# A hybrid attention and expert block on one Trainium2 core: all 40 modulation weight tiles of the first part are multiplied and summed by VectorE, and none by Pool

## Chip, cores and metric

The kernel runs on one core of one Trainium2 chip. The metric is the device time of one execution in microseconds; the kernel before was timed in three runs, and their median stands for it. One more execution was profiled, and all rows come from that one.

## What is computed

The reference is one block on 256 tokens of width 1024. Cut to its main lines:

```
ada = silu(c) @ w_ada + b_ada                     # w_ada: 1024 x 6144, the modulation
shift1, scale1, gate1, shift2, scale2, gate2 = split(ada, 6)
h = rms_norm(x) * (1 + scale1) + shift1
qa, ka, va, qb, kb, vb = split(h @ w_in)
mixed = concat(rms_norm(windowed_attention(qa, ka, va)), rms_norm(neighbourhood_attention(qb, kb, vb)))
x = x + gate1 * (mixed @ w_out)
h2 = rms_norm(x) * (1 + scale2) + shift2
x = x + gate2 * peer(h2)                          # 8 heads choose 16 of 16384 experts for each token
out = rms_norm(x) * final_g
```

Everything is float32. `ada` is a product of one vector with a matrix: six parts of eight column groups, 48 tiles of 128 outputs by 1024 inputs.

## The kernel before

**Tiles and parts.** Features lie on the 128 partitions, eight chunks of them, and tokens run along the free axis. A modulation tile has an output on each partition and the 1024 inputs along the free axis. The first part of the kernel makes 40 of the 48 tiles (all but gate2, whose eight tiles come late in the second part), the input projection (18 weight tiles), attention in eight pairs of heads, the output projection (8 tiles), the second norm and the first products of the expert queries. The second part does the remaining queries, the choice of experts, and runs over 128 tiles of the first and 128 tiles of the second expert matrix; beside these, for 96 tokens, single expert rows are fetched by indirect DMAs of Pool's queue.

**A modulation tile** (`load_ada`, lines 592 to 607). `ca` holds silu(c), the same 1024 numbers on every partition. On VectorE one `scalar_tensor_tensor` with `accum_out` multiplies the tile by `ca` and leaves the sum in one column of `ada` (lines 606 and 607). For the 15 tiles in the table `ON_POOL` (line 39), Pool multiplies the tile by `ca` in place (line 598), and ScalarE then adds up the row by an `activation` with `accum_out` (line 601). The 15 belong to gate1, scale2 and shift2, so the 16 tiles of scale1 and shift1 are on VectorE already.

**Weight tiles of the projections.** `load_w` loads a tile, ScalarE rounds it to its high half (line 626), and VectorE or Pool subtracts that from it for the low half (`lo`, line 630). TensorE multiplies the halves in three terms (lines 442 and 806).

**What sets the order.** The first part is written as jobs with the engines they may run on, each with a cost, what it depends on and which buffers it takes. A planner (`plan`, `forward`, `backward`) orders them: a list scheduler that is run 300 times with disturbed priorities from a fixed seed, and of which the order with the earliest end of TensorE is kept. Jobs with several engines are the split's subtraction (VectorE or Pool), evictions from PSUM (ScalarE or VectorE: the projection at line 851 or 853, turned values at 870 or 872, turned probabilities at 1007 or 1009, attention's output at 1032 or 1034), the weighing of the softmax (line 982 for VectorE and Pool, 979 for ScalarE) and additions (540 and 1081, VectorE or Pool). Each engine's instructions are then written down in that order, and every engine works its own queue strictly in order. Weights are loaded by SP's queue, in the planner's order, into 8 buffers of one kind and 9 of another; a load stands at the head of SP's queue until its buffer is free. In the second part the order is written by hand, with a count of each engine's assumed time for VectorE's side work.

**Other lines that are named below.** 945: VectorE adds the bias to the scores and takes the extreme from PSUM. 962, 968 and 973: small sums and reciprocals of the softmax. 949: ScalarE's exponential. 750: the sums of squares over the partitions on TensorE. 1077: the output projection times gate and norm, from PSUM. 1557 and 1507: the products of the two expert matrices.

Of the kernel before, what the change touches and what calls it, by code (L numbers as in the profile page):

```python
# [12 lines left out]
AF = mybir.ActivationFunctionType  # L13
# [3 lines left out]
P = 128  # L17
D = 1024
NC8 = 8
# [16 lines left out]
NCST = _o  # L36

SHIFT1, SCALE1, GATE1, SHIFT2, SCALE2, GATE2 = range(6)
ON_POOL = {(GATE1, 0), (GATE1, 2), (GATE1, 3), (GATE1, 5), (GATE1, 7), (SCALE2, 0), (SCALE2, 1), (SCALE2, 2), (SCALE2, 4), (SCALE2, 5), (SCALE2, 6), (SHIFT2, 1), (SHIFT2, 2), (SHIFT2, 3), (SHIFT2, 4)}
RAW = 4  # L40
SETTLE = 6.0
SETS = (64, 32)
# [17 lines left out]
LO_POOL = 1  # L60
# [5 lines left out]
def kernel(ctx: ExitStack, tc: tile.TileContext, xT, crow, vecs, cst, w_ada, w_in, w_out,  # L66
# [11 lines left out]
    V, S, PE, G = nc.vector, nc.scalar, nc.tensor, nc.gpsimd  # L78
# [7 lines left out]
    ada = keep.tile([P, 6, 8], F32, name="ada")  # L86
# [3 lines left out]
    cs = keep.tile([P, 8], F32, name="cs")  # L90
# [54 lines left out]
    def add(alts, *deps, take=(), free=(), lag=0.0, after=None, rows=P):  # L145
        return Job(alts, deps, take, free, lag, after, rows)
# [174 lines left out]
    MM = 0.1095  # L321
# [16 lines left out]
    tiles = {}  # L338
# [125 lines left out]
    ca = carve(D)  # L464
# [52 lines left out]
    def silu(y, x):  # L517
        S.activation(y, x, AF.Exp, scale=-1.0)
        V.tensor_scalar(y, y, 1.0, None, op0=ALU.add)
        V.reciprocal(y, y)  # L520
        V.tensor_mul(y, y, x)

    silu(c8t[:8], c8[:8])
    for w, part in ((0, SCALE1), (1, SCALE2)):
        a0 = VEC["b_ada"][0] + part * 8
        V.scalar_tensor_tensor(gb[:, w, :], vec[:, a0:a0 + 8], 1.0, v_("g2" if w else "g1"),
                               op0=ALU.add, op1=ALU.mult)
# [19 lines left out]
    cas = []  # L547
    for w in range(2):
        key = ("ca", w)
# [6 lines left out]
        m = add([("pe", 0.86, spread_c)], take=[("bank", key)], rows=8)  # L556
# [33 lines left out]
    column = {}  # L590

    def load_ada(part, c):
        key = ("ada", part, c)
        m = load(w_ada[part, c], key)
        col = ada[:, part, c:c + 1]
        if (part, c) in ON_POOL:
            def mul():
                G.tensor_mul(tiles[key], tiles[key], ca)

            def total():  # L600
                S.activation(tiles[key], tiles[key], AF.Copy, accum_out=col)

            m = add([("pool", 2.3, mul)], m, *cas)
            column[part, c] = add([("act", 1.04, total)], m, free=[key])
        else:
            column[part, c] = add([("dve", 1.15, lambda: V.scalar_tensor_tensor(
                tiles[key], tiles[key], 1.0, ca, op0=ALU.mult, op1=ALU.mult, accum_out=col))], m, *cas, free=[key])

    halved = {}
# [4 lines left out]
    def load_w(kind, i):  # L614
        key = ("w", kind, i)
        m = load(SRC[kind][i], key)
        hkey = ("h", kind, i)
        held_key[kind, i] = hkey
        if (kind, i) in WHOLE or kind == "q" and i < NQ:
            halved[kind, i] = whole[kind, i] = m  # L620
            held_key[kind, i] = key
            return

        def high():
            halves[kind, i] = new_halves(got(hkey))
            S.activation(halves[kind, i][0], tiles[key].rearrange("p (c n) -> p c n", n=P), AF.Copy)

        def low(e):
            hi, lo = halves[kind, i]
            e.tensor_sub(lo, tiles[key].rearrange("p (c n) -> p c n", n=P), hi.bitcast(F32))  # L630

        a = add([("act", 0.95, high)], m, take=[("split", hkey)])
        halved[kind, i] = add([("dve", 1.14, lambda: low(V))] + [("pool", 2.3, lambda: low(G))] * LO_POOL, a, free=[key])


    lscr = dram.tile([8, 512], F32, name="lscr")
# [1 line left out]
    def line_mm():  # L638
        PE.matmul(take_bank("line").rearrange("p a b -> p (a b)")[:8, :], t5s[:32], onehs[:32], start=True, stop=True)

    m = add([("pe", 0.86, line_mm)], take=[("bank", "line")], rows=32)
    m = add([("dve", 0.65, lambda: V.tensor_add(line[:8], tiles["line"].rearrange("p a b -> p (a b)")[:8, :], maska[:8]))],
            m, free=["line"])
# [122 lines left out]
    m = None  # L766
    for i in range(4):
        a = add([op("act", c_act(512), S.activation, sq[:, 2 * i:2 * i + 2, :], xs[:, 2 * i:2 * i + 2, :],
                    AF.Square)], xin[i])
        if i:  # L770
            a = add([op("dve", c_dve(512), V.tensor_add, sq[:, 0:2, :], sq[:, 0:2, :], sq[:, 2 * i:2 * i + 2, :])], a, m)
        m = a
    m = add([op("dve", c_dve(256), V.tensor_add, sq[:, 0, :], sq[:, 0, :], sq[:, 1, :])], m)
    m = ssum("n1", sq[:, 0, :], m)
# [3 lines left out]
    for c in range(NC8):  # L778
        x = add([op("pool", c_pool(256), G.tensor_mul, xr[:, c, :], xs[:, c, :], ny),
                 op("dve", c_dve(256), V.tensor_mul, xr[:, c, :], xs[:, c, :], ny)], scaled)  # L780
        a = add([op("dve", 0.08, V.scalar_tensor_tensor, mod[:, 0, c:c + 1], ada[:, SCALE1, c:c + 1], v_("g1", c),
                    gb[:, 0, c:c + 1], op0=ALU.mult, op1=ALU.add)], column[SCALE1, c])
# [33 lines left out]
    m = None  # L816
    for c in range(NC8):
        if KT == 16:
            for k in range(2):
                m = kouter(("in", 2 * c + k), [(c, n) for n in range(8 * k, 8 * k + 8)], m, hready[c])  # L820
            continue
        i = 3 * (c // 2) + c % 2
        m = kouter(("in", i), [(c, n) for n in range(8)], m, hready[c])
        if c % 2:
            m = kouter(("in", i + 1), [(b, n) for b in (c - 1, c) for n in range(8, 12)], m, hready[c], hready[c - 1])
# [53 lines left out]
    for i in range(KT, 18):  # L879
        key = ("in", i)  # L880

        def win(i=i, key=key):
            products_of(take_bank(key)[:, 0, :], operands(("in", i), xr), ALL)

        m = add([("pe", tile_cost(("in", i)), win)], halved["in", i], *hready, take=[("bank", key)],
                free=[held_key["in", i]])
# [12 lines left out]
    for u in range(8):  # L899
        q, k, vn, bias, j = pair_names(u)  # L900
# [18 lines left out]
        def score(u=u, q=q, k=k, skeys=skeys):  # L919
            ps = [take_bank(x) for x in skeys]  # L920
            for b in range(2 if u < 4 else 4):
# [10 lines left out]
                take=[("bank", x) for x in skeys] + [("pb", pkey)], rows=64 if GA else 50)  # L932
        previous = chain(previous, s, PACE)
        for b in ((0, 2, 1, 3) if GA else range(4)):
# [17 lines left out]
            a = add([("dve", 0.42 if GA else 0.285, shifted)], s, bias_in, free=[skeys[b % 2 if GA else 0]])  # L952
# [4 lines left out]
        if GA:  # L957
# [12 lines left out]
            a = add([("dve", 0.15, sink1)], *ttrs)  # L970
            a = add([("act", 0.2, sink2)], a)
            last = [add([("dve", 0.1, sink3)], a, *exps)]
        a = add([("dve", 0.15, lambda st_=st_: V.reciprocal(st_()[:, 3, :], st_()[:, 1, :]))], *last)
# [17 lines left out]
        for half, norm in enumerate(norms):  # L991
# [12 lines left out]
            def kept(eng, tkey=tkey, ckey=ckey):  # L1004
# [3 lines left out]
                else:  # L1008
# [4 lines left out]
                             take=[("ptb", ckey)], free=[tkey]))  # L1013
# [624 lines left out]
def _layout(np, i):  # L1638
    def cols(v):
        return v.reshape(-1, P).T  # L1640

    def tiles(w):
        return w.reshape(8, P, -1, P).transpose(2, 1, 0, 3).reshape(-1, P, D)

    pa = np.array([j + 4 * s for j in range(4) for s in range(2)])
    fa = (pa[:, None] * 64 + np.arange(64)[None]).reshape(-1)
    vec = np.concatenate([
        cols(i["c"][0]),
        i["b_ada"][0].reshape(6, 8, P).transpose(2, 0, 1).reshape(P, 48),
        cols(i["norm1_g"][0]), cols(i["norm2_g"][0]), cols(i["final_g"]),  # L1650
        cols(i["out_norm_a"][0][fa]), cols(i["out_norm_b"][0]),
        np.broadcast_to(i["sink_a"][0][pa][None], (P, 8)),
    ], axis=1)
    w_in = i["w_in"][0]
    order = [np.arange(512, 640)] + [fa[j * P:(j + 1) * P] for j in range(4)] + [np.arange(640, 768)]
    for j in range(4):
        for s in range(3):
            order.append(768 + 512 * s + j * P + np.arange(P))
    w_in = tiles(w_in[:, np.concatenate(order)]).reshape(18, P, 8, P)
    first = []  # L1660
    for cp in range(4 if KT == 12 else 0):
        for c in (2 * cp, 2 * cp + 1):
            first.append(w_in[0:8, :, c].transpose(1, 0, 2))
        first.append(w_in[8:12, :, 2 * cp:2 * cp + 2].transpose(1, 2, 0, 3).reshape(P, 8, P))
    for c in range(8 if KT == 16 else 0):
        for k in range(2):
            first.append(w_in[8 * k:8 * k + 8, :, c].transpose(1, 0, 2))
    w_in = np.concatenate([np.stack(first), w_in[KT:]]).reshape(18, P, D)
    w_out = i["w_out"][0]
    w_out = np.concatenate([w_out[:512][fa], w_out[512:]], axis=0)  # L1670
    w_out = w_out.reshape(2, 4, P, 4, 2, P).transpose(0, 3, 2, 4, 1, 5).reshape(8, P, D)
    rpb = np.stack([i["rpb_b"][0].reshape(4, 2, 465)[:, :, 108 + 31 * r:264 + 31 * r] for r in range(4)])
    rpb = rpb.transpose(2, 0, 1, 3).reshape(-1)
    return {
        "xT": i["x"][0].T.reshape(8, P, T).transpose(1, 0, 2),
        "crow": i["c"].reshape(8, P),
        "vecs": vec,
        "cst": _constants(np),
        "w_ada": i["w_ada"][0].T.reshape(6, 8, P, D),
        "w_in": w_in,  # L1680
        "w_out": w_out,
        "w_query": tiles(i["w_query"][0]),
        "t5": i["t5_table"][:, pa],
        "rpb": rpb,
        "skT": i["sub_keys"][0].reshape(16, P, P).transpose(2, 0, 1),
        "uT": i["u_experts"][0].reshape(NE, P, 8, P).transpose(0, 3, 2, 1).reshape(NE, P, D),
        "uE": i["u_experts"][0],
        "vE": i["v_experts"][0],
    }
# [20 lines left out]
```

## Time and profile before

| | us |
|---|---|
| Median of three runs | 851.04 (849.75 to 851.42) |
| Profiled execution | 850.8 |
| Its span, first to last instruction | 849.0 |
| TensorE busy in it | 775.2 |
| VectorE busy | 593.1 |
| ScalarE busy | 268.0 |
| Pool busy | 330.6 |

The span is what the rows of the trace add up to; the execution's own time lies 1.8 us over it. The busy times are averages over stages with different limits, so a stage has to be read by itself. A VectorE row's time is that of the instruction from its start to its end, with what it waited for inside the engine counted in; waiting for a semaphore before the start is counted as idle.

### The profile page before, as it was taken

What the parts mean: (1) busy time and instruction counts of PE and PEld (TensorE: products, weight loads), DVE (VectorE), ACT (ScalarE), POOL (GpSimd) and SP (SyncE); (2) the same over time, 40 slices, a digit from 0 to 9 for tenths busy, and PEclk for the clock granted to TensorE, in tenths of its full rate; (3) what the DMA queues carried; (4) which work ended last, traced back from release to release, by engine and by line L of the source; (5) the groups of instructions that cost most, each with busy time, mean ns of one, the idle gap of its engine ahead of it and who ended that gap; (6) DMA issues with size and microseconds to landing.
All of it is one profiled execution on the core that took longest, in us unless ns stands there. A gap on an engine that the chain in (4) does not pass through costs nothing.

```text
span 849.0 us, 15375 instructions
## 1 busy us (share of the span) xinstructions
PE 775.2 (91%) x5846; PEld 753.9 (89%) x5846; DVE 593.1 (70%) x1308; ACT 268.0 (32%) x741; POOL 330.6 (39%) x271
## 2 busy tenths in 40 slices
PE   3998786789799999999999999999999989899894
PEld 1997575689799999999999999999999988899893
DVE  6999999887677999569998775644435444453534
ACT  4456675456231112179876521000000000000003
POOL 2545686456314436412233233533333333332300
PEclk9999998999999999999999999999999999999997
DMA  8995666095768999999999999999999999999951
GB/s 328 408 328 206 223 227 234 0 348 202 259 229 297 392 413 395 416 413 361 359 378 374 401 371 416 415 412 416 415 416 415 414 415 416 415 413 418 414 205 50
DMA packets 81212, 289.27 MB, mean 341 GB/s; under 512 B 9281, under 2 KB 10825, under 8 KB 81010
## 3 DMA queue, kind: packets, MB, share of 16 engines
q1 hardware_dynamic: 36352, 125.60, 38.5%
q0 software_dynamic: 27776, 100.79, 30.2%
q10 hardware_dynamic: 17010, 61.89, 18.4%
q8 instruction: 46, 0.75, 0.4%
q14 instruction: 28, 0.23, 0.1%
HBM read 287.18 MB, written 1.07 MB: 340 GB/s over the span
## 4 chain that ended last, share of the span: by engine, by line
PE 34%; DMA 28%; issue 5%; DVE 3%; POOL 3%; ACT 0%; DVEq 0%; ACTq 0%; POOLq 0%
PE b L1507 27%; DMA row<-in_vE,big 24%; PE b L1557 4%; DMA raw<-in_vE,big 3%; PE b L1474 2%; DVE accg L1443 1%; POOL row L1421 1%; DMA row<-in_uT 1%; POOL raw L1421 1%; DMA row<-in_vE 1%; PE b L1342 1%; PE b L1562 0%; POOL big L1421 0%; DVE big L1443 0%; POOL lo L398 0%
## 5 line engine op out<-in xcount | busy, mean ns | idle before, releaser
L1507 PE MATMUL b<-big 128*128 128x160 f32 x928 | 134.3, 302 | 4.0 <-ACT big L1489 4.0
L1557 PE MATMUL b<-big 128*128 128x160 f32 x944 | 131.0, 299 | 5.0 <-DMA big<-in_vE 4.2
L1557 PEld LDWEIGHTS b<-big 128*128 128x128 f32 x944 | 129.0, 190 | 5.7 <-DMA big<-in_vE 4.7
L1557 PE MATMUL b<-big,row 128*128 128x160 f32 x864 | 125.5, 305 | 7.4 <-DMA row<-in_vE 7.4
L1507 PEld LDWEIGHTS b<-big 128*128 128x128 f32 x928 | 128.4, 191 | 4.2 <-ACT big L1489 4.2
L1557 PEld LDWEIGHTS b<-big,row 128*128 128x128 f32 x864 | 121.8, 194 | 8.1 <-DMA row<-in_vE 4.3
L1507 PE MATMUL b<-big,row 128*128 128x160 f32 x752 | 106.6, 300 | 0.0
L1507 PEld LDWEIGHTS b<-big,row 128*128 128x128 f32 x752 | 103.0, 190 | 0.0
L540 ACT ACTIVATE big<-xs 128x256 f32<-128x256 f32 (+1 forms) x20 | 9.1, 457 | 283.8 <-DVE xs L540 273.8
L1421 POOL DMA_INDIRECT row<-in_vE,big x48 | 49.9, 1039 | 88.0 <-DVE accg L1443 58.5
L1443 DVE SCALAR_TENSOR_TENSOR accg<-row,big,accg 128x1024 f32<-128x1024 f32 x32 | 41.2, 1286 | 51.2 <-DMA row<-in_vE,big 48.4
L442 PE MATMUL b<-hb,hi 128*128 128x256 f32 x432 | 65.5, 295 | 1.9 <-DVE hb L540 1.9
L1421 POOL DMA_INDIRECT raw<-in_vE,big x36 | 37.2, 1033 | 70.5 <-DVE accg L1443 45.5
L1421 POOL DMA_INDIRECT row<-in_uE,big x37 | 39.6, 1071 | 61.9 <-DVE big L1493 29.2
L1489 ACT ACTIVATE big<-b 128x160 f32<-128x160 f32 (+23 forms) x110 | 29.0, 266 | 104.3 <-PE b L1507 85.4
L442 PEld LDWEIGHTS b<-hb,hi 128*128 128x128 f32 x432 | 58.2, 199 | 3.9 <-DVE hb L540 2.1
L1421 POOL DMA_INDIRECT raw<-in_uE,big x34 | 34.5, 1015 | 63.6 <-DVE raw L1434 29.0
L1443 DVE SCALAR_TENSOR_TENSOR accg<-raw,big,accg 128x1024 f32<-128x1024 f32 x23 | 29.6, 1285 | 38.2 <-DMA raw<-in_vE,big 38.1
L1465 ACT ACTIVATE oh<-iota,ebf 128x128 f16<-128x128 f16 x160 | 51.0, 394 | 13.2 <-PE b L1474 9.4
L1421 POOL DMA_INDIRECT big<-in_uE,big x25 | 25.7, 1028 | 70.1 <-issue 29.3
L442 PE MATMUL b<-hb,lo 128*128 128x256 f32 x216 | 33.1, 291 | 6.6 <-DVE lo L630 5.0
L442 PEld LDWEIGHTS b<-hb,lo 128*128 128x128 f32 x216 | 28.7, 194 | 8.6 <-DVE lo L630 5.6
(212 smaller groups left out, 1381.2 us busy)
## 6 DMA issues: line engine op xcount, KB each, us to landing
big<-in_uT SPq DMA_DIRECT2D x36, 512.0 KB
big<-in_w_ada SPq DMA_DIRECT2D x33, 512.0 KB
big<-in_vE SPq DMA_DIRECT2D x31, 512.0 KB
row<-in_vE SPq DMA_DIRECT2D x29, 512.0 KB
big<-in_vE ACTq DMA_DIRECT2D x28, 512.0 KB
row<-in_vE ACTq DMA_DIRECT2D x25, 512.0 KB
row<-in_uT ACTq DMA_DIRECT2D x24, 512.0 KB
row<-in_uT SPq DMA_DIRECT2D x23, 512.0 KB
```

The lines of the kernel that those rows point to most:

```text
L442: PE.matmul(ps, w[:, wc, :], r[:, rc, :], start=(n == 0), stop=(n == last))
L540: return (e, cost, lambda: f(*a, **k))
L1342: PE.matmul(px[:, c * P:(c + 1) * P], rep[:, 4 * i + c, :], ident, start=True, stop=True)
L1421: G.indirect_dma_start(row, None, uE if k < GT else vE, bass.IndirectOffsetOnAxis(ap=cidx[:, k % GT:k % GT + 1], axis=0))
L1443: V.scalar_tensor_tensor(accg[w], row, ag[:, k - GT:k - GT + 1], accg[w], op0=ALU.mult, op1=ALU.add)
L1465: S.activation(oh1[:, k, :], iota1, AF.Square, scale=-1.0, bias=ebf[:, t0 + k:t0 + k + 1])
L1474: PE.matmul(pg[:, k, :], pr[:, i, :, k], oh1[:, k, :], start=(i == 0), stop=(i == 1))
L1489: S.activation(gz[:, e, t:], ps[:, 0, t:ND], AF.Gelu_apprx_tanh)
L1507: PE.matmul(ps[:, 0, 0:ND], w[:, c, :], h2[:, c, GT:], start=(c == 0), stop=(c == NC8 - 1))
L1557: PE.matmul(acc[c][:, 0, GT:], w[:, c, :], gz[:, e, :], start=(e == 0), stop=(e == NE - 1), skip_group_check=True)
```

## The change

The table of Pool's tiles goes, and with it the branch that used Pool and ScalarE. In its place stands a table of tiles for TensorE, which is empty, so that all 40 tiles take the branch of VectorE. The cost that the planner assumes for a product on VectorE goes from 1.15 to 1.3 us, and for a split's subtraction from 1.14 to 1.22 us. A column form of silu(c), `cs`, is computed at the start: three instructions of 128x8 on VectorE and one on ScalarE, which nothing reads as long as the table is empty. Cut to its core:

```diff
-ON_POOL = {(GATE1, 0), (GATE1, 2), (GATE1, 3), (GATE1, 5), (GATE1, 7), (SCALE2, 0), (SCALE2, 1), (SCALE2, 2), (SCALE2, 4), (SCALE2, 5), (SCALE2, 6), (SHIFT2, 1), (SHIFT2, 2), (SHIFT2, 3), (SHIFT2, 4)}
+ON_PE = set()
...
     silu(c8t[:8], c8[:8])
+    silu(cs, v_("c"))
...
-        if (part, c) in ON_POOL:
-            def mul():
-                G.tensor_mul(tiles[key], tiles[key], ca)
-
-            def total():
-                S.activation(tiles[key], tiles[key], AF.Copy, accum_out=col)
-
-            m = add([("pool", 2.3, mul)], m, *cas)
-            column[part, c] = add([("act", 1.04, total)], m, free=[key])
+        if (part, c) in ON_PE:
...
         else:
-            column[part, c] = add([("dve", 1.15, lambda: V.scalar_tensor_tensor(
+            column[part, c] = add([("dve", 1.3, lambda: V.scalar_tensor_tensor(
                 tiles[key], tiles[key], 1.0, ca, op0=ALU.mult, op1=ALU.mult, accum_out=col))], m, *cas, free=[key])
...
-        halved[kind, i] = add([("dve", 1.14, lambda: low(V))] + [("pool", 2.3, lambda: low(G))] * LO_POOL, a, free=[key])
+        halved[kind, i] = add([("dve", 1.22, lambda: low(V))] + [("pool", 2.3, lambda: low(G))] * LO_POOL, a, free=[key])
```

The planner starts from other jobs and costs and so writes the whole first part in another order. The changed file's lines lie one or two higher: what was at 606 is at 608, 630 at 632, 982 at 984.

Pool's queue from the neighbourhood bias on (line 660), before the change; the rows of line 598 are the products, `raw` and `big` the buffers of the weight tile:

```order
L660 TENSOR_TENSOR big<-big 128x4x128 x3
L598 TENSOR_TENSOR big<-big 128x1024 x2
L598 TENSOR_TENSOR raw_667<-raw_667,big 128x1024
L598 TENSOR_TENSOR raw_724<-raw_724,big 128x1024
L598 TENSOR_TENSOR big<-big 128x1024
L982 TENSOR_TENSOR big<-big 128x2x256 x2
L598 TENSOR_TENSOR raw_884<-raw_884,big 128x1024
L598 TENSOR_TENSOR big<-big 128x1024 x3
```

The same place after it (line 662 is the bias), with two split subtractions, a weighing and small subtractions and additions:

```order
L662 TENSOR_TENSOR big<-big 128x4x128 x3
L632 TENSOR_TENSOR lo_668<-big,hi_667 128x1024
L632 TENSOR_TENSOR lo_883<-raw_826,hi_882 128x1024
L984 TENSOR_TENSOR big<-big 128x2x256
L541 TENSOR_TENSOR hb<-big,hb 128x256
L541 TENSOR_TENSOR big<-big 128x256 x2
```

The products are gone from Pool, and what follows them in its queue has moved up.

VectorE's queue in the attention of the first group, before the change, where a softmax's sums, its reciprocal and its weighing stand between evictions (851) and two products (606):

```order
L606 SCALAR_TENSOR_TENSOR raw_714,ada<-raw_714,big 128x1024
L851 TENSOR_SCALAR big<-b_689 128x256
L968 TENSOR_TENSOR big<-big 128x4
L973 RECIPROCAL big<-big 128x4
L982 TENSOR_TENSOR big<-big 128x2x256 x2
L630 TENSOR_TENSOR lo_804<-big,hi_803 128x1024
L851 TENSOR_SCALAR big<-b_735 128x256
```

The same place after it, with the reciprocal and the weighing of a pair of heads (975 and 984):

```order
L632 TENSOR_TENSOR lo_927<-big,hi_926 128x1024
L608 SCALAR_TENSOR_TENSOR raw_920,ada<-raw_920,big 128x1024
L608 SCALAR_TENSOR_TENSOR raw_924,ada<-raw_924,big 128x1024
L975 RECIPROCAL big<-big 128x4
L984 TENSOR_TENSOR big<-big 128x2x256
L608 SCALAR_TENSOR_TENSOR big,ada<-big 128x1024
L970 TENSOR_TENSOR big<-big 128x4
```

Products now stand before and after each step of the softmax, and the evictions of the projection have left VectorE's queue here.

## Rows read from the trace of the kernel before

**Rows 1.** Windows: length, busy us (instructions) of each engine, clock, DMA share, GB/s.
```profile
0.00:62.00 62.00, 46.35 (x316) 42.88 (x316) 53.40 (x86) 29.56 (x47) 27.11 (x24) 1.00 0.95 358
62.00:128.00 66.00, 52.83 (x418) 43.97 (x414) 65.25 (x136) 46.39 (x126) 45.41 (x20) 0.95 0.63 219
128.00:177.40 49.40, 35.30 (x241) 31.87 (x242) 46.19 (x83) 24.42 (x54) 26.50 (x20) 0.86 0.39 137
177.40:485.00 307.60, 301.38 (x2405) 298.19 (x2404) 250.88 (x795) 145.38 (x447) 119.14 (x98) 0.99 0.91 351
485.00:849.00 364.00, 339.34 (x2475) 337.03 (x2473) 177.39 (x212) 22.29 (x69) 112.49 (x110) 0.98 0.94 379
```
The five engines stand in the order PE, PEld (weight loads), DVE, ACT, POOL.

**Rows 2.** Waits of TensorE, 62 to 170 us: total us, times, longest.
```profile
PE b L750 <- DVE big L540: 7.6, 2, 4.1
PE b L442 <- DVE lo L630: 5.0, 3, 2.2
```

**Rows 3.** Waits of TensorE, 177 to 849 us.
```profile
PE b L1557 <- DMA row<-in_vE: 7.4, 3, 3.6
PE b L1557 <- DMA big<-in_vE: 4.2, 2, 2.3
```

**Rows 4.** Timeline of VectorE: start us, length us, line, operation, count.
```profile
35.70 1.22 DVE L606 SCALAR_TENSOR_TENSOR big<-big 128x1024 f32<-128x1024 f32 x1
36.85 1.22 DVE L630 TENSOR_TENSOR lo<-big,hi 128x1024 fp32r<-128x1024 f32 x1
...
65.05 2.98 DVE L606 SCALAR_TENSOR_TENSOR big<-big 128x1024 f32<-128x1024 f32 x1
...
76.04 0.28 DVE L962 TENSOR_TENSOR big<-big,vec 128x2 f32<-128x2 f32 x2
...
86.55 0.69 DVE L982 TENSOR_TENSOR big<-big 128x512 f32<-128x512 f32 x1
...
95.33 2.38 DVE L962 TENSOR_TENSOR big<-big,vec 128x2 f32<-128x2 f32 x2
...
129.74 3.39 DVE L630 TENSOR_TENSOR lo<-raw,hi 128x1024 fp32r<-128x1024 f32 x1
133.05 0.86 DVE L1077 SCALAR_TENSOR_TENSOR big<-b,ada,big 128x256 f32<-128x256 f32 x2
...
157.86 0.42 DVE L1081 TENSOR_TENSOR xs<-xs,big 128x256 f32<-128x256 f32 x1
```

**Rows 5.** Timeline of Pool at two of these places.
```profile
94.29 7.97 POOL L598 TENSOR_TENSOR big<-big 128x1024 f32<-128x1024 f32 x3
...
129.23 6.16 POOL L598 TENSOR_TENSOR big<-big 128x1024 f32<-128x1024 f32 x2
```

**Rows 6.** Groups by form, 0 to 180 us: count, busy us, mean ns, idle before.
```profile
L598 POOL TENSOR_TENSOR big<-big 128x1024 f32<-128x1024 f32 x11 | 32.0, 2933 | 4.9 <-DMA big<-in_w_ada 4.9
L598 POOL TENSOR_TENSOR raw<-raw,big 128x1024 f32<-128x1024 f32 x4 | 11.5, 2882 | 0.0
L630 POOL TENSOR_TENSOR lo<-raw,hi 128x1024 fp32r<-128x1024 f32 x3 | 7.2, 2414 | 2.6 <-ACT hi L626 2.6
L1081 POOL TENSOR_TENSOR xs<-xs,big 128x256 f32<-128x256 f32 x6 | 4.4, 762 | 5.4 <-DVE big L973 4.3 <-DVE big L1077 1.1
L601 ACT ACTIVATE big<-big 128x1024 f32<-128x1024 f32 x11 | 11.5, 1050 | 0.8 <-POOL big L598 0.8
```

**Rows 7.** Groups by form of VectorE's evictions, 0 to 180 us.
```profile
L851 DVE TENSOR_SCALAR big<-b 128x256 f32<-128x256 f32 x8 | 3.1, 412 | 0.0
L1007 DVE COPY big<-b 128x512 f32<-128x512 f32 x4 | 2.6, 676 | 0.0
L1032 DVE TENSOR_SCALAR big<-b,vec 128x256 f32<-128x256 f32 x5 | 2.4, 471 | 0.0
```

**Rows 8.** Waits of Pool and of SP's queue, 60 to 170 us.
```profile
POOL big L598 <- DMA big<-in_w_ada: 4.9, 1, 4.9
SPq L586 <- DVE lo L630: 21.1, 7, 4.8
```

More of the change, by code (lines that the diff above doesn't have):

```diff
@@ L595, in load_ada, with products_c @@
         col = ada[:, part, c:c + 1]
-        if (part, c) in ON_POOL:
-            def mul():
-                G.tensor_mul(tiles[key], tiles[key], ca)
-            def total():
-                S.activation(tiles[key], tiles[key], AF.Copy, accum_out=col)
-            m = add([("pool", 2.3, mul)], m, *cas)
-            column[part, c] = add([("act", 1.04, total)], m, free=[key])
+        if (part, c) in ON_PE:
+            def products_c():
+                w = tiles[key].rearrange("p (c n) -> p c n", n=P)
+                pc = take_bank(("adac", part, c))
+                for k in range(NC8):
+                    PE.matmul(pc[:, 0, 0:1], w[:, k, :], cs[:, k:k + 1], start=(k == 0), stop=(k == NC8 - 1))
+            m = add([("pe", 16 * MM, products_c)], m, take=[("bank", ("adac", part, c))], free=[key])
+            column[part, c] = add([("act", 0.25, lambda: S.activation(
+                col, tiles["adac", part, c][:, 0, 0:1], AF.Copy))], m, free=[("adac", part, c)])
         else:
-            column[part, c] = add([("dve", 1.15, lambda: V.scalar_tensor_tensor(
+            column[part, c] = add([("dve", 1.3, lambda: V.scalar_tensor_tensor(
                 tiles[key], tiles[key], 1.0, ca, op0=ALU.mult, op1=ALU.mult, accum_out=col))], m, *cas, free=[key])
@@ L1673, in _layout @@
     rpb = rpb.transpose(2, 0, 1, 3).reshape(-1)
+    ada = i["w_ada"][0].T.reshape(6, 8, P, D).copy()
+    for part, c in ON_PE:
+        ada[part, c] = ada[part, c].T.reshape(8, P, P).transpose(1, 0, 2).reshape(P, D)
     return {
@@ L1678, in _layout @@
         "cst": _constants(np),
-        "w_ada": i["w_ada"][0].T.reshape(6, 8, P, D),
+        "w_ada": ada,
         "w_in": w_in,
```

## The prediction

> **What bounds the kernel now.** I read the windows first, because the kernel has stages with different limits, then who waits for whom, then single instructions of VectorE and Pool side by side.
>
> The windows [rows 1] cut the 849.0 us span into five stretches. From 0 to 62 us the input projection keeps TensorE at work (46.35 us of 62, and most of the rest is its start). From 62 to 177.4 us, the attention, output projection and second norm, TensorE is busy 52.83 of 66.00 us and 35.30 of 49.40 us, ScalarE 46.39 and 24.42 us, DMA has a share of 0.63 and 0.39, and VectorE is busy 65.25 of 66.00 and 46.19 of 49.40 us. So VectorE sets the pace of that stage. The waits agree: the longest waits of TensorE there end on VectorE [rows 2]. From 177.4 us on, TensorE is busy 301.38 of 307.60 us up to 485, and after that TensorE and DMA (share 0.94) run nearly level; its longest waits there are on loads, 7.4 and 4.2 us [rows 3].
>
> What follows 177.4 us is issued in the same order before and after the change: on TensorE, VectorE, ScalarE and Pool the two programs read alike from about the last early query products on, apart from buffer numbers. All of it hangs on the end of the planned part: the loads of the expert rows need the indices, and the first tiles of the expert weights need the areas that the planned part frees. I therefore carry a gain or loss at 177.4 us to the end one for one, and the question is only what VectorE does between 62 and 177 us.
>
> VectorE is not slow there by its own work. A multiply-and-sum of 128x1024 takes 1.22 us at 35.70 us, where Pool is idle, and the next instruction starts 1.15 us after it; the split's subtraction at 36.85 us also takes 1.22 us [rows 4]. At 65.05 us, beside a product on Pool, the same multiply-and-sum takes 2.98 us; at 129.74 us a subtraction takes 3.39 us; at 95.33 us two additions of 128x2, which take 0.28 us at 76.04 us, take 2.38 us. Pool is in the middle of its weight products at 94.29 and at 129.23 us [rows 5]. But at 133.05 us, still beside Pool's second product, two instructions that read PSUM keep their 0.43 us each [rows 4]. So a VectorE instruction with two SBUF inputs stands still until Pool's instruction is over, and one that reads PSUM does not.
>
> **The change part by part.** *Added to VectorE.* Fifteen multiply-and-sums of 128x1024. At 1.15 us from start to start plus some 0.05 us where its sum is read out, 1.2 us each: 15 x 1.2 = 18.0 us. None of it has cover while VectorE is full.
>
> *Taken from Pool.* Fifteen products, 32.0 + 11.5 = 43.5 us [rows 6]. Pool's own time costs nothing; what counts is what it held up. Along VectorE's timeline I took each instruction that overlaps one of these fifteen and set it against the shortest of its own form. There are 12 that are clearly longer, the first at 65.05 us, 2.98 us instead of 1.22, the last at 129.74 us, 3.39 instead of 1.22; the pair at 95.33 us gives 2.1 [rows 4]. Together they are 20.8 us longer, 1.4 us for each product. I take -20.8 us. The Trainium skill, SBUF, "Who interferes with whom", calls this an exclusive lock; if VectorE met it at every product for its whole length, fifteen times the 2.4 us of Pool's shortest products would be 35 us and the sum 14 us lower; the trace shows 21, since not every product meets such an instruction.
>
> *Taken from ScalarE.* Fifteen sums of 128x1024, eleven of them 11.5 us together [rows 6]. ScalarE is busy 70% and 49% of the two stretches [rows 1], so this is no gain in itself. It is what lets the planner move other work there.
>
> *Moved by the planner.* The order of the changed kernel has all 40 products on VectorE, but thirteen evictions from PSUM fewer there: five at the input projection (412 ns), three at the output of attention (471 ns), two of 512 columns (676 ns) and three at the turned values (two of 512 columns, one of 256) [rows 7], together 6.6 us. Three weighings of softmax (0.69 us each, as at 86.55 us) and four additions to the residual (0.42 us, as at 157.86 us) go as well [rows 4], 3.8 us. The sum is 10.4 us of busy time; consecutive instructions overlap by some 0.07 us, so 20 of them are worth 9.0 us: -9.0 us. It is a gain as long as ScalarE, which takes most of it, is not later with them than VectorE was. In the input stage three subtractions of the split go to Pool and three small products come back; TensorE is the bound there, and I put both at nothing.
>
> *What Pool gets instead.* Four residual additions at 762 ns [rows 6] and one more split subtraction, which took 2.4 us on Pool [rows 6]: 5.4 us. Held against VectorE like the old products it is between 0 and +5.4 us; I take the middle, since Pool's products did so for about half of their time: +2.7 us.
>
> *A new wait.* Pool could stand at a late weight tile and only its own queue stood behind it: once it waited 4.9 us for one [rows 8]. Now VectorE stands there, with the score evictions and the split's subtractions queued behind it, and TensorE waits for these. The tile is late when its buffer came free late, and SP waited for buffers in this stage for 21.1 us on the split's subtractions alone [rows 8]. Bounds: 0 if the planner has put every product behind its landing, +4.9 us if that one wait is met in full. I take the middle, +2.4 us. The silu of three tiny instructions at the start lies in VectorE's idle time before the first sums and costs nothing; uncovered it would be about 0.5 us.
>
> Sum: 18.0 - 20.8 - 9.0 + 2.7 + 2.4 = **-6.7 us**. The profiled execution took 850.8 us, 0.24 us under the median of 851.04; against the median this gives **844.3 us**.
>
> **The rivals.** *Slower: the work counts and the standing still remains.* VectorE gets 18.0 us more and loses 9.0. The 20.8 us go only if nothing else on Pool takes the products' place. But Pool keeps 99.0 - 43.5 = 55.5 us of other work in these stretches [rows 1, 6], and with the products gone it starts that work as soon as its inputs are there, which is while VectorE is busy. If only a quarter of the 20.8 us goes, the sum is 18.0 - 5.2 - 9.0 + 2.7 = +6.5, without the landing wait, so about 857; below 11.7 us regained it is a loss. For it speaks that VectorE has no idle time; against it that the 12 long instructions each lie on one of these products. The Trainium skill, Perfetto Trace Analysis, "Optimizing Scalar/DVE Operations", says that offloading from a saturated VectorE, even to GPSIMD, may make sense, which speaks against undoing it, and adds that between these two it might not help, because of the port they share. Rows bear the second half out.
>
> *No change: the landing waits.* Two waits of the 4.9 us kind on VectorE instead of the half that I took add 7.4 us and eat the gain: 851 or 852. For it speaks SP's wait for buffers; against it that VectorE frees a tile in 1.2 us where Pool and ScalarE took 2.9 + 1.05 us, so that loads start earlier.
>
> *A larger gain.* If neither the landing wait nor the new work on Pool costs anything, the sum is 18.0 - 20.8 - 9.0 = -11.8 us, 839; and if VectorE then also stands still less beside the rest of Pool's work, since Pool is idle more of the time, -15 us, 836.
>
> *That the change does not do what it says* can be left out: the order has 40 products on VectorE and none on Pool.
>
> **How the numbers follow.** The forecast, 844.3, gets 0.57, the slower rival (857) 0.17, no change (851) 0.14, the larger gain (836 to 839) 0.12. A difference of 0.2%, 1.7 us, is about what a measurement of this kernel can tell from no change. Faster: 0.57 + 0.12 = 0.69; same 0.14; slower 0.17. The range goes from 836, the end of the larger gain, to 856, which leaves out the upper half of the slower case and a little at the bottom.
>
> **What would show it.** Right: multiply-and-sums at 1.2 to 1.5 us in the mean over 40; VectorE's busy time up to 177 us smaller by 5 to 10 us though it has 15 more large instructions; the third stretch ending near 170 us; from there on equal stretches. Wrong: VectorE instructions of 2 to 3 us beside Pool's split subtractions and residual additions as often as before (the slower rival); idle time of VectorE that ends on loads of the modulation weights (no change); TensorE waiting longer for ScalarE's evictions, which would undo the -9.0; or an end of the planned part that is earlier without the kernel's end following, which would take down the one-for-one rule.

## The result and the profile after

The changed kernel takes 838.53 us in the median (835.98 to 840.05), against 851.0 for the kernel before: a ratio of 0.9853 (0.9825 to 0.9881), 12.5 us faster. The profiled execution took 839.29 us with a span of 837.5 us, 11.5 us under the span before. It lies inside the range of the prediction, 5.8 us under the forecast of 844.3 and within the 836 to 839 us of the rival with the larger gain.

The windows of the kernel after, cut where its stages are cut in [rows 1]; the third ends 12 us earlier, where the remaining queries begin:

```profile
0.00:62.00 62.00, 44.66 (x305) 40.86 (x306) 55.90 (x85) 26.88 (x40) 29.80 (x24) 1.00 0.93 352
62.00:128.00 66.00, 53.05 (x422) 45.09 (x422) 61.51 (x147) 44.14 (x122) 14.90 (x10) 0.90 0.82 297
128.00:165.40 37.40, 31.68 (x253) 28.84 (x250) 33.73 (x78) 21.96 (x56) 19.75 (x21) 0.95 0.16 57
165.40:473.00 307.60, 300.98 (x2400) 298.00 (x2400) 251.31 (x797) 145.42 (x446) 118.08 (x98) 0.99 0.91 349
473.00:837.50 364.50, 341.68 (x2481) 339.53 (x2480) 177.24 (x212) 22.33 (x69) 116.09 (x111) 0.97 0.94 379
```

From the third window's end on, the two kernels are level: 307.60 us with 300.98 us of TensorE work against 301.38, and 364.5 us against 364.0. The whole gain is in the first part. There VectorE is busy 55.90 + 61.51 + 33.73 = 151.1 us, against 53.40 + 65.25 + 46.19 = 164.8 us in [rows 1]: 13.7 us less, though it does 15 more large instructions. Pool's 99.0 us have become 64.5. TensorE's granted clock, a mean of stretches at 1.2 and at 2.4 GHz, is 0.94 of full speed over these three windows before and 0.95 after, so the clock does not make the difference.

The groups of VectorE's large instructions after, up to the remaining queries: count, busy us, mean ns, idle before them. Line 608 is the multiply-and-sum, 632 the split's subtraction:

```profile
L608 DVE SCALAR_TENSOR_TENSOR big<-big 128x1024 f32<-128x1024 f32 x27 | 36.8, 1375 | 0.0
L608 DVE SCALAR_TENSOR_TENSOR raw<-raw,big 128x1024 f32<-128x1024 f32 x13 | 17.7, 1366 | 0.0
L632 DVE TENSOR_TENSOR lo<-raw,hi 128x1024 fp32r<-128x1024 f32 x12 | 17.3, 1450 | 0.0
L632 DVE TENSOR_TENSOR lo<-big,hi 128x1024 fp32r<-128x1024 f32 x11 | 14.1, 1281 | 0.2 <-ACT hi L628 0.2
```

Forty multiply-and-sums of 1.37 us on average, inside the 1.2 to 1.5 us that were named ahead. None of them waits: the idle time before them is 0.0, so no late load held VectorE up.

The longest waits of VectorE after, 60 to 166 us (total us, times, longest), name ScalarE and Pool, and no load:

```profile
DVE hb L541 <- ACT hb L541: 2.0, 1, 2.0
DVE big L717 <- ACT big L714: 1.7, 1, 1.7
DVE big L541 <- POOL big L541: 1.4, 1, 1.4
```

One place got slower. At the start of the input projection Pool now subtracts a split, and VectorE, which has to finish the norm, stands beside it. In the new order VectorE also comes to that step of the norm 2.1 us later. Timeline of Pool after, below it that of VectorE (729 is the last step of the reciprocal root), and last the same step before the change (727):

```profile
18.43 3.09 POOL L632 TENSOR_TENSOR lo<-big,hi 128x1024 fp32r<-128x1024 f32 x1 [14.84 <-ACT hi L628]
...
19.24 2.56 DVE L729 SCALAR_TENSOR_TENSOR big<-big 128x256 f32<-128x256 f32 x1
...
17.11 0.42 DVE L727 SCALAR_TENSOR_TENSOR big<-big 128x256 f32<-128x256 f32 x1
```

TensorE's first product of the projection, which started at 21.19 us before, starts at 23.39 us:

```profile
23.39 2.08 PE L808 MATMUL b<-hb,hi 128*128 128x256 f32 x8 [10.89 <-ACT hb L541]
```

### The profile page after: what moved, and what is told of

The parts are those of the page before. It is cut to its first block, busy times and chain, and to the rows that moved or that the text cites. A ratio compares the mean times of both kernels' runs of the same rounds, so it can differ in the third digit from the quotient of the medians.

```text
span 837.5 us, 15369 instructions
## 1 busy us (share of the span) xinstructions
PE 772.0 (92%) x5846; PEld 752.3 (90%) x5846; DVE 579.7 (69%) x1317; ACT 260.7 (31%) x733; POOL 298.6 (36%) x263
## 4 chain that ended last, share of the span: by engine, by line
PE 35%; DMA 28%; issue 5%; POOL 3%; DVE 3%; ACT 0%; DVEq 0%; ACTq 0%; POOLq 0%
PE b L1509 27%; DMA big<-in_vE,big 13%; DMA row<-in_vE,big 12%; PE b L1559 4%; PE b L1476 2%; DMA raw<-in_vE,big 2%; POOL row L1423 1%; DVE accg L1445 1%; POOL raw L1423 1%; DMA row<-in_uT 1%; DVE big L1445 0%; PE b L1344 0%; PE b L1564 0%; POOL big L1423 0%; POOL lo L398 0%
## 5 line engine op out<-in xcount | busy, mean ns | idle before, releaser
L1509 PE MATMUL b<-big 128*128 128x160 f32 x928 | 135.5, 303 | 4.6 <-ACT big L1491 4.6
L1559 PE MATMUL b<-big 128*128 128x160 f32 x944 | 132.8, 302 | 4.6 <-DMA big<-in_vE 3.8
L1559 PEld LDWEIGHTS b<-big 128*128 128x128 f32 x944 | 130.7, 192 | 5.4 <-DMA big<-in_vE 4.3
L1509 PEld LDWEIGHTS b<-big 128*128 128x128 f32 x928 | 129.6, 193 | 4.8 <-ACT big L1491 4.8
L1445 DVE SCALAR_TENSOR_TENSOR accg<-row,big,accg 128x1024 f32<-128x1024 f32 x32 | 41.1, 1284 | 52.0 <-DMA row<-in_vE,big 50.5
L1423 POOL DMA_INDIRECT raw<-in_vE,big x36 | 38.9, 1080 | 69.5 <-DVE accg L1445 42.3
L442 PE MATMUL b<-hb,hi 128*128 128x256 f32 x432 | 62.6, 287 | 0.0
L442 PEld LDWEIGHTS b<-hb,hi 128*128 128x128 f32 x432 | 55.7, 191 | 0.8 <-issue 0.7
L808 PE MATMUL b<-hb,hi 128*128 128x256 f32 x192 | 27.5, 297 | 11.5 <-ACT hb L541 11.2
L1445 DVE SCALAR_TENSOR_TENSOR big<-row,big 128x1024 f32<-128x1024 f32 x16 | 20.6, 1285 | 24.4 <-DMA row<-in_vE,big 24.3
```

The lines of the kernel that those rows point to most:

```text
L442: PE.matmul(ps, w[:, wc, :], r[:, rc, :], start=(n == 0), stop=(n == last))
L808: PE.matmul(tiles["acc", n // 2][:, n % 2, :], w[:, b, :], r[:, c, :], start=(c == 0 and t == 0 and n % 2 == 0), stop=(c == NC8 - 1 and t ...
L1423: G.indirect_dma_start(row, None, uE if k < GT else vE, bass.IndirectOffsetOnAxis(ap=cidx[:, k % GT:k % GT + 1], axis=0))
L1445: V.scalar_tensor_tensor(accg[w], row, ag[:, k - GT:k - GT + 1], accg[w], op0=ALU.mult, op1=ALU.add)
L1509: PE.matmul(ps[:, 0, 0:ND], w[:, c, :], h2[:, c, GT:], start=(c == 0), stop=(c == NC8 - 1))
L1559: PE.matmul(acc[c][:, 0, GT:], w[:, c, :], gz[:, e, :], start=(e == 0), stop=(e == NE - 1), skip_group_check=True)
```

## The experiments

All ratios are against the kernel before, timed beside each run (medians 849.6 to 850.0 us there). What was asked: is it Pool's products standing in VectorE's way, or the planner's other order, or only the spread that any new order has?

**The engine alone, in the order of before.** Pool's product becomes VectorE's multiply-and-sum where it stood, and ScalarE's sum goes:

```diff
 def mul():
-    G.tensor_mul(tiles[key], tiles[key], ca)
+    V.scalar_tensor_tensor(tiles[key], tiles[key], 1.0, ca, op0=ALU.mult, op1=ALU.mult, accum_out=col)
 def total():
-    S.activation(tiles[key], tiles[key], AF.Copy, accum_out=col)
+    pass
```

> The order of the kernel before, kept row for row, but its 15 Pool products are done by VectorE at the places of Pool's products, with the sum in the same instruction; Pool's products and ScalarE's sums are gone. Theory (VectorE stands still beside Pool's products): VectorE gets 15 x 1.2 = 18.0 us more and loses about 21 us of standing still, so about -3 us against before, 848 (844 to 852, since VectorE may now wait at a late tile). Rival (Pool's products cost VectorE little, and the gain is the planner's other order): +10 to +18 us, 861 to 869.

Measured: 845.25 us, ratio 0.9946 (0.9927 to 0.9965). The windows of this run, up to the remaining queries:

```profile
0.00:62.00 62.00, 47.27 (x322) 43.52 (x323) 54.01 (x89) 29.45 (x48) 26.19 (x23) 1.00 0.96 360
62.00:172.00 110.00, 88.11 (x651) 76.04 (x650) 105.63 (x243) 55.84 (x149) 28.99 (x25) 0.89 0.53 190
```

VectorE's busy time is 54.01 + 105.63 = 159.6 us, 5.2 us less than before with 15 instructions more. At 1.22 us these are 18.3 us, so 23.5 us of standing still have gone. The rival's +10 to +18 us is out.

**The same with ScalarE's load kept.** ScalarE copies each of the 15 tiles into an area that nothing reads:

```diff
 def total():
-    pass
+    S.activation(scr, tiles[key], AF.Copy)
```

> The order of the kernel before with its 15 Pool products on VectorE (as in the run before, 845.3), but ScalarE keeps 15 row passes: where it summed a tile, it copies that tile into an area that nothing reads. So against before only Pool's products go over to VectorE and ScalarE's load stays. Theory (the swap of engines gains by itself, ScalarE was not in the way in this order): 843 to 848. Rival (the 4 us of that run came from ScalarE's freed time): 849 to 853.

Measured: 843.40 us, ratio 0.9936 (0.9916 to 0.9956), the interval overlapping that of the run without the copies. In this order ScalarE's sums cost nothing, and the swap from Pool to VectorE gains by itself, 6 us here and 4 us in the run without the copies.

**The engine alone, in the order of after.** The 15 products go back to Pool, with ScalarE's sums, and each stays where VectorE had it in the order:

```diff
+if (part, c) in ON_POOL:
+    G.tensor_mul(tiles[key], tiles[key], ca)
+    S.activation(tiles[key], tiles[key], AF.Copy, accum_out=col)
+else:
     V.scalar_tensor_tensor(tiles[key], tiles[key], 1.0, ca, ..., accum_out=col)
```

> The order of the changed kernel, kept, but the 15 products that were Pool's before are done by Pool and summed by ScalarE at the places where VectorE does them. Theory (standing still): VectorE loses 18.0 us of work and gets 21 us or more of standing still, and ScalarE gets 15 sums in front of its exponentials: 845 to 856. Rival (the order makes the gain, not the engine): 838 or less, as VectorE has 18 us less to do.

Measured: 852.98 us, ratio 1.0040 (1.0028 to 1.0052), 14.5 us over the changed kernel though VectorE has 18 us less to do. The order of after is no better than that of before once Pool does the products. The windows of this run, up to the remaining queries:

```profile
0.00:62.00 62.00, 44.62 (x305) 40.90 (x306) 55.98 (x84) 26.82 (x40) 32.56 (x25) 1.00 0.94 352
62.00:178.60 116.60, 88.61 (x667) 75.84 (x667) 91.57 (x197) 81.48 (x208) 70.39 (x46) 0.88 0.52 187
```

VectorE's busy time is 55.98 + 91.57 = 147.6 us, only 3.6 less than in the changed kernel, so some 14 us of standing still came back, less than the 21 I expected. Its idle time went from 14.3 to 31.1 us, and this waiting is the larger part of the loss: this run does not show the price of the standing still alone. VectorE stands behind ScalarE; its two longest such waits:

```profile
DVE hb L542 <- ACT hb L542: 8.5, 1, 8.5
...
DVE lo L639 <- ACT hi L635: 7.6, 2, 5.1
```

**The assumed costs alone.** First the kernel before with the new costs, then the changed kernel with the old ones:

```diff
-"dve", 1.15
+"dve", 1.3
...
-"dve", 1.14
+"dve", 1.22
```

> The kernel before with its 15 products on Pool, but with the changed kernel's assumed costs (1.3 us for a product on VectorE, 1.22 us for a split subtraction), so that the planner writes another order. Theory (the products on Pool are what costs): 845 to 855, no gain beyond the spread of orders. Rival (the new costs make the better order): about 839.

Measured: 849.27 us, ratio 0.9992 (0.9975 to 1.0009). No gain.

> The changed kernel, all 40 products on VectorE, with the old assumed costs (1.15 and 1.14 us). Theory (the products on Pool are what costs): the gain stays, 835 to 843. Rival (the new costs make the better order): about 848 to 851.

Measured: 842.83 us, ratio 0.9918 (0.9887 to 0.9950). More than half of the gain stays, by the ratios. The new costs without the change gain nothing; some 4 us depend on which order the planner happens to write.

**Pool's presence alone.** The changed kernel in its own order; behind each of the 15 products Pool multiplies the tile once more, into an area that nothing reads:

```diff
 V.scalar_tensor_tensor(tiles[key], tiles[key], 1.0, ca, ..., accum_out=col)
+if (part, c) in ON_POOL:
+    G.tensor_mul(scr, tiles[key], ca)
```

> The changed kernel in its own order, and behind each of the 15 products that were Pool's before Pool multiplies the same tile once more into an area that nothing reads (15 extra products, no other work changed; the tile's buffer is held until Pool is done). Theory (VectorE stands still beside Pool): 1.4 us for each product, as in the trace of before, so some +20 us, 852 to 862. Rival (Pool's products do not hold VectorE up): +0 to +3 us from the buffers alone, 838 to 842.

Measured: 866.51 us, ratio 1.0189 (1.0168 to 1.0209), 28 us over the changed kernel and more than expected. The windows of this run, up to the remaining queries:

```profile
0.00:62.00 62.00, 44.52 (x304) 40.73 (x305) 55.81 (x85) 26.79 (x40) 29.16 (x24) 1.00 0.94 351
62.00:192.70 130.70, 90.75 (x668) 78.21 (x667) 118.34 (x225) 66.97 (x178) 76.41 (x46) 0.83 0.49 167
```

VectorE's busy time is 55.81 + 118.34 = 174.2 us against 151.1, with the same instructions: 23 us longer, 1.5 us for each product of Pool. The split's subtractions show it best, 1831 and 1650 ns against 1450 and 1281 in the changed kernel:

```profile
L639 DVE TENSOR_TENSOR lo<-raw,hi 128x1024 fp32r<-128x1024 f32 x12 | 21.9, 1831 | 0.5 <-ACT hi L635 0.5
...
L639 DVE TENSOR_TENSOR lo<-big,hi 128x1024 fp32r<-128x1024 f32 x11 | 18.1, 1650 | 0.2 <-ACT hi L635 0.2
```

The remaining queries begin 27.3 us later than in the changed kernel, so some 4 us more are idle time of VectorE. What sets them is not separated: Pool's real work now stands behind the extra products in its queue, and TensorE's granted clock is lower too (0.83 in the second window, so more of it at 1.2 GHz). TensorE's waits on Pool in this run:

```profile
PE b L759 <- POOL big L544: 7.1, 1, 7.1
...
PE b L443 <- POOL lo L639: 5.3, 1, 5.3
...
PE b L1008 <- POOL big L991: 4.0, 1, 4.0
```

**The same on ScalarE.** The extra work is a copy on ScalarE, which holds the tile's buffer too, though for a shorter time than Pool's product:

```diff
-    G.tensor_mul(scr, tiles[key], ca)
+    S.activation(scr, tiles[key], AF.Copy)
```

> As the run with 15 extra products on Pool, but the extra work is a copy of the same tile on ScalarE (15 x 1.05 us), which holds the buffer in the same way. Theory: ScalarE does not hold VectorE up, so only what lies behind the copies in ScalarE's queue is later: +0 to +5 us, 838 to 844. Rival (it is the held buffers that cost, not the port): as much as with Pool, 850 or more.

Measured: 850.13 us, ratio 0.9997 (0.9981 to 1.0014), 11.6 us over the changed kernel; I had expected at most 5. But VectorE does not stand still: its busy time up to the remaining queries is 55.73 + 96.81 = 152.5 us, 1.4 more than in the changed kernel.

```profile
0.00:62.00 62.00, 43.95 (x303) 40.27 (x304) 55.73 (x85) 26.77 (x40) 30.15 (x24) 1.00 0.94 351
62.00:176.60 114.60, 90.35 (x670) 77.38 (x669) 96.81 (x222) 79.91 (x193) 33.14 (x31) 0.86 0.54 190
```

The loss is waiting instead, VectorE for the high half of the split that stands behind the copies in ScalarE's queue (0.2 us in the changed kernel):

```profile
DVE lo L639 <- ACT hi L635: 8.0, 6, 2.4
```

So an instruction on Pool lengthens VectorE's instructions, and one on ScalarE does not; but in the order of after the copies hold up what stands behind them in ScalarE's queue. ScalarE is not full there (79.91 of 114.60 us): its copies wait for VectorE's products of the same tiles, 12.1 us in all:

```profile
ACT big L614 <- DVE raw L612: 7.6, 5, 2.7
...
ACT big L614 <- DVE big L612: 4.5, 2, 2.9
```

**Less on Pool.** The changed kernel with `LO_POOL = 0`, so that all split subtractions of the planned part are VectorE's:

> The changed kernel with the split subtractions of the planned part on VectorE alone (5 fewer on Pool; the planner writes a new order). If a Pool subtraction of 2.4 us holds VectorE up for about as long as VectorE takes to do it itself (1.2 us), no change: 835 to 841. If the slower start of the input projection (2.2 us later than before) comes from the one subtraction on Pool there, 834 to 837. If VectorE's own work decides, +3 to +6 us: 842 to 845.

Measured: 833.82 us, ratio 0.9801 (0.9779 to 0.9823), a little better than my best case. TensorE's first product of the projection starts at 19.09 us:

```profile
19.09 2.08 PE L808 MATMUL b<-hb,hi 128*128 128x256 f32 x8 [4.39 <-ACT hb L541]
```

That is 4.3 us earlier than in the changed kernel. But the remaining queries begin only 2.4 us earlier (163.18 against 165.62 us), and the two spans differ by 2.0 us, 835.5 against 837.5. Nor does an early start make a fast run elsewhere: with the old costs TensorE starts at 16.68 us and the kernel takes 842.8 us, and in the fastest run, the next one, it starts at 22.55 us. So the 4.7 us between the medians are not shown to come from the start, and they are no more than the spread of orders below.

**Almost nothing on Pool.** Beside `LO_POOL = 0`, Pool is struck from every other choice of engine:

```diff
-ADDERS = [("dve", c_dve, V), ("pool", c_pool, G)]
+ADDERS = [("dve", c_dve, V)]
```

and likewise from the products of the first norm, the weighing and the residual.

> The changed kernel with nothing on Pool in the planned part but the neighbourhood bias and two casts: split subtractions, the 256-column additions, subtractions and products and the weighing are VectorE's (or ScalarE's) alone, also the products of the final norm. VectorE gets 5 x 1.2 + 37 x 0.34 = 18 to 19 us more than in the changed kernel and loses up to the 31 us that its instructions are longer than the shortest of their form there. Theory (standing still beside Pool costs more than the work): 826 to 836. Rival (the small ones on Pool are worth their price, VectorE becomes the bound): 838 to 846.

Measured: 827.30 us, ratio 0.9731 (0.9696 to 0.9766), the best of all and 11 us better than the changed kernel. Its windows and its multiply-and-sums:

```profile
0.00:62.00 62.00, 45.65 (x318) 42.52 (x319) 53.65 (x101) 30.23 (x49) 7.80 (x11) 1.00 0.97 367
62.00:158.60 96.60, 80.74 (x654) 70.20 (x654) 90.28 (x244) 64.83 (x177) 2.19 (x2) 0.93 0.59 216
```

```profile
L608 DVE SCALAR_TENSOR_TENSOR big<-big 128x1024 f32<-128x1024 f32 x27 | 32.8, 1219 | 0.0
...
L608 DVE SCALAR_TENSOR_TENSOR raw<-raw,big 128x1024 f32<-128x1024 f32 x13 | 15.7, 1217 | 0.0
```

With Pool quiet the 40 instructions take 1.22 us each, the shortest time of [rows 4], and VectorE's busy time is 143.9 us, though it does some 18 us more work than in the changed kernel. The planned part ends 6.9 us earlier than there; the other 5.8 us of the 12.7 us between the two spans come after it, where the only difference in the program is the products of the final norm. The traces place 3.7 us of these at the very end. Between TensorE's last product and the end of the span lie 12.2 us in the changed kernel and 8.5 us here. Timeline of TensorE after, then in this run, and last the closing rows (DRAIN) of Pool's queue in the changed kernel, with the shortest, median and longest in ns and the first and last start:

```profile
823.61 1.69 PE L752 MATMUL b<-big 128*128 128x256 f32 x6
...
814.61 1.69 PE L752 MATMUL b<-big 128*128 128x256 f32 x6
...
L1710 POOLq DRAIN  x3: 51/92/8921, 827.8 to 837.2; - x3
```

In the changed kernel Pool does two products of the final norm, and the longest of these rows, of 8.92 us, lasts until 836.7 us, while SP's queue, which stores the result, is through at 833.7 us. Here Pool has nothing to do there, and the kernel ends 0.8 us after SP's queue is through. The other 2 us lie in the stretch of the expert products, whose length varies from 607.3 to 613.1 us over all fourteen traces.

**The spread of orders.** Another seed for the kernel before and for the changed one, and a third for before:

> The kernel before with another seed of the planner, so another order of the same work. If orders spread little: 845 to 857. Rival (the difference of 12.5 us is no more than the spread between orders): anything from 838 to 863, and the changed kernel with other seeds overlaps it.

Measured: 853.98 us, ratio 1.0038 (1.0018 to 1.0058).

> The changed kernel with another seed of the planner (the same as in the run of before with another seed, which took 854). Theory (the products leaving Pool make the gain in any order): 836 to 846, at least 8 us under before with that seed. Rival (spread between orders): 848 or more.

Measured: 844.83 us, ratio 0.9934 (0.9913 to 0.9956), 9.2 us under before with the same seed, but in the upper part of what I expected.

> The kernel before with a third seed. Spread of before's orders as seen so far is 849 to 854; theory: 847 to 857. Rival (spread between orders as large as the change): below 843 or above 860.

Measured: 846.40 us, ratio 0.9960 (0.9944 to 0.9976), a little under what I expected.

With these, four orders with products on Pool took 851.0, 849.3, 854.0 and 846.4 us, 850.2 on average, and three with all products on VectorE 838.5, 842.8 and 844.8 us, 842.1 on average. The averages are 8 us apart. The ranges do not overlap, but the nearest two orders are only 1.6 us apart and their intervals overlap, so seven orders alone do not settle it. The rival that only the spread between orders was seen falls by the swap in an unchanged order, which gained 4 to 6 us; and about 4 of the 12.5 us are what this one order happens to be better than its like.

## Why the prediction was right, point by point

*The bound and the one-for-one rule*: right. The remaining queries begin at 165.62 us instead of 177.36, 11.7 us earlier, and the span is 11.5 us shorter. Over the other runs the part behind that point kept its length to within 3 us or so of 672 us; only the run with almost nothing on Pool went below, to 666. Of the signs named ahead, the mean of the multiply-and-sums came as said; VectorE's busy time fell by 13.7 us, more than the 5 to 10 named, and the third stretch ended at 165 us, not near 170.

*Added to VectorE, +18.0 us*: right; an undisturbed instruction takes 1.22 us still.

*Standing still beside Pool's products, -20.8 us*: right in kind, 2.7 us short in size. In the order of before, where nothing else moves, it was -23.5 us; Pool's 15 extra products put 23 us back. The trace of before held the rest too: with five instructions beside these products that are 0.3 to 0.6 us longer than the shortest of their form, the same working gives 23.8 us.

*ScalarE's sums, no gain in themselves*: right for the order of before (843.4 with them, 845.3 without), wrong for the order of after, where 15 passes of ScalarE cost 11.6 us. That run shows what the place of such passes in ScalarE's queue costs, behind VectorE's products; what ScalarE's room is worth by itself no run shows. The prediction had said that it lets the planner move other work, and priced the moved work alone.

*Moved by the planner, what Pool gets instead, and the landing wait: -9.0 + 2.7 + 2.4*: this is where the size was off. From the run with the engine swapped in the old order to the changed kernel, VectorE's busy time falls by another 8.5 us (159.6 to 151.1); the sum had -9.0 + 2.7 = -6.3. To part the two, I set each VectorE instruction before the remaining queries against the shortest of its form in the traces of these runs. The sum of the shortest times falls by 11.6 us (150.0 to 138.4): the prediction's -9.0 missed six small instructions of 256 columns that also went to Pool. What the instructions take beyond it rises by 2.8 us (28.7 to 31.5), close to the +2.7, but not where I looked for it: 6.6 us more in the input stage, 2.7 more up to 128 us, and 6.5 less after that, where four split subtractions of Pool had stood. The landing wait of +2.4 us did not come at all: no wait of VectorE there ends on a load. Its idle time before the remaining queries still rose by 1.7 us, from 12.5 to 14.2.

In the other direction, TensorE starts 2.2 us later in the input stage, which I had put at nothing. I had called TensorE the bound there and forgotten that it first waits for the norm on VectorE. The norm's last step begins 2.1 us later in the new order and takes 2.1 us longer beside Pool's subtraction; what of this reaches the end of the kernel is not shown.

*The spread of orders* was missing from the working. The sum of -6.7 us fits the 8 us between the averages better than the 12.5 us of this order. The forecast was right about the change, and the range, not the sum, covered the order. That the measured time lies as far down as 838.5 us is in part the luck of one order.

*The rivals.* Slower (the standing still remains): excluded, 23.5 us of it went with the products in the unchanged order. In the changed kernel as a whole what the instructions take beyond the shortest fell from 50.5 to 31.5 us, so much of it does remain, beside Pool's other work. No change (late loads): excluded by VectorE's waits. The larger gain, 836 to 839 with a chance of 0.12, met the number, and only partly for its own reason: the landing wait was absent, but Pool's new work was not free and VectorE did not stand still less beside the rest of it. The Trainium skill, Perfetto Trace Analysis, "Optimizing Scalar/DVE Operations", was weighed ahead; of its two halves this kernel bears out only the second, that moving work between VectorE and GPSIMD might not help, and goes beyond it: here it costs 4 to 6 us in an unchanged order.

## What to carry to other kernels

When VectorE is full, look at the length of its instructions and not only at their number: where the same form takes 1.2 us at one place and 3 us at another, look what Pool does beside it, and price a helper on Pool by what VectorE loses there, here 1.4 to 1.6 us for each product, of 2.4 us at its shortest, more than the 1.2 us that VectorE needs to do it. The same accounting holds for the split subtractions and small additions: without them on Pool, VectorE's busy time fell by 7 us more though it had some 18 us more to do. Of the 11 us that this gave, nearly 4 lie at the very end of the kernel, and the order was a single one. And where a planner writes the order, measure two or three orders of each version before a difference of 4 us is put down to the change.

## What I had not expected of the hardware

Being short does not protect an instruction. After the change two instructions with a single element on each partition take 2.2 and 2.4 us at 46.57 and 48.73 us, beside Pool's two split subtractions of 45.41 us on; elsewhere they take 0.15 and 0.21 us. VectorE's timeline after:

```profile
46.57 2.23 DVE L541 TENSOR_TENSOR ada<-ada,vec 128x1 f32<-128x1 f32 x1
48.73 2.43 DVE L541 SCALAR_TENSOR_TENSOR mod<-ada,vec,gb 128x1 f32<-128x1 f32 x1
```

And all of this is counted as busy time: in the windows of before VectorE looks 99% full between 62 and 128 us [rows 1], while more than 20 us of it are standing still.
